# Routing steps tied to the low part of their tile, twelve instead of eight up tiles split by GpSimd

## The chip, the cores and the metric

One core of a Trainium2 chip runs the whole program in one launch. The metric is device time in microseconds (us), the median of several executions; less is better. The engines are named as the profile names them: PE is TensorE (matmuls), DVE is VectorE, ACT is ScalarE, POOL is GpSimd, SP issues the loads. PEld is PE's weight load.

## The reference

A decoder trunk of two layers on 256 tokens with 1024 channels: layer 0 mixes by retention, layer 1 by sparse attention, and each layer ends with a product-key expert network ("peer") of 16384 experts. The change is in that network alone:

```python
q = (xc @ w_q).reshape(T, 8, 2, 128)
s = einsum('thcd,hcnd->thcn', q, sub_keys)      # 8 heads, 2 halves, 128 keys
sv, si = top_k(s, 16)
comb = (sv[:, :, 0, :, None] + sv[:, :, 1, None, :]).reshape(T, 8, 256)
cv, ci = top_k(comb, 16)
eidx = i1 * 128 + i2        # i1, i2: si taken at ci // 16 and ci % 16
w = softmax(cv)
a = gelu(einsum('td,thkd->thk', xc, u_tab[eidx])) * w
y = einsum('thk,thkd->td', a, v_tab[eidx])
```

## The kernel before

All matrix products are made in three passes. Each fp32 operand is split into a high part, rounded by ACT (`hi`, line 98), and a low part, the difference `lo = raw - hi` (function `minus`, line 105), and `mm3` sums high by high, high by low and low by high.

The expert network doesn't gather. It goes through all 128 tiles of 128 experts: `up(i)` multiplies the tokens with tile i of `u_tab` (24 matmuls of 256 columns), a gelu makes `g`, DVE multiplies it by the dense routing weight `W`, and `down(i)` multiplies the result with tile i of `v_tab`. The tiles come in two halves of 64; in each, `RING` = 60 up tiles run first. The network runs twice, once a layer; below these are the first and the second network.

In the first 60 up tiles of the first half, DVE and ACT also finish the routing:

- `queries` and `first` (before the up tiles): scores and the two top-16 lists of each head; `second` (lines 593 to 604): the top 16 of their sums. All are DVE work.
- `weights` (line 649 on DVE, then line 651, an exp on ACT that needs a table load before it, and one back for the gelu): the softmax's numerators, issued after up tile `FINISH[0]`.
- `ranks` (lines 618 to 643): which keys the winners have. 18 steps of small and large DVE instructions, dealt out over the up tiles of `RANKS`.
- `normalised` (lines 656 to 659), then `finish` after up tile `FINISH[1]`: six transposes on PE, copies by ACT.
- `dense` (lines 689 to 700): 34 steps dealt out over the up tiles of `DENSE`; DVE makes one-hot rows, PE multiplies them, ACT copies them into `W`.

`UPLO` says for each up tile which engine makes its two low parts: "pp" is POOL, "dd" is DVE. `hi` and `lo` have four buffers each, two tiles' worth, so ACT and the engine of the low part run at most two tiles ahead of PE; the raw tiles have five.

PE's order is the order in which the code is written. On DVE, ACT and POOL a scheduler orders the instructions by its own estimates, except inside `manual_schedule`, and `issue_after(x)` keeps what stands in it behind instruction x in that order. Each engine works its list strictly in order.

Of the kernel before, what the change touches and what calls it, by code (L numbers as in the profile page):

```python
# [16 lines left out]
OP = mybir.AluOpType  # L17
# [7 lines left out]
HALF = 64  # L25
RING = 60
TB = 8
UPLO = (["pp"] * 8 + ["dd"] * 52, ["dd"] * 60)
DENSE = (24, 59), (0, 56)
FINISH = (8, 23)  # L30
RANKS = (9, 22)
STEPS = [1] * 4 + [2, 0, 0] * 5 + [2, 1] * 6 + [2]
WSCALE = 2.0 ** 14
C_ADAB, C_KVB, C_LNG, C_LNB, C_B1, C_PE, C_END = 0, 96, 112, 144, 176, 180, 212
# [3 lines left out]
def trunk(ctx, tc, a, out, dbg=None, stop=None):  # L38
    nc = tc.nc
# [24 lines left out]
    state = {}  # L64
# [4 lines left out]
    def x_tile():  # L69

        state["x"] = const.tile([P, 2, D], FT, tag="x", name="x")
        return state["x"]
# [29 lines left out]
            nc.gpsimd.tensor_scalar(dst, src, 1.0, 0.0, op0=OP.mult, op1=OP.add)  # L102

    def minus(eng, dst, x, y):
        (nc.vector if eng == "dve" else nc.gpsimd).tensor_tensor(dst, x, y, op=OP.subtract)  # L105

    def part512(raw, n, lo):

# [49 lines left out]
    def drain(g, n=10 ** 9):  # L158
        for _ in range(n):
            if next(g, StopIteration) is StopIteration:  # L160
                return
# [346 lines left out]
    def peer(l, h2, g, bg, end=lambda norm: iter(())):  # L508
        V = nc.vector
        with ExitStack() as s:  # L510
# [104 lines left out]
            def ranks(tt):  # L615

                for c in range(2):
                    V.tensor_copy(sf[:, tt, c], si[:, tt, :, c].rearrange("p h j -> p j h"))

                p, q, r0, r1 = cf[:, tt, 0], cf[:, tt, 1], rr[:, tt, 0], rr[:, tt, 1]  # L620
                V.tensor_copy(p, ci[:, tt].rearrange("p h k -> p k h"))
                V.tensor_scalar(ci[:, tt], ci[:, tt], 3, None, op0=OP.logical_shift_right)
                V.tensor_copy(r0, ci[:, tt].rearrange("p h k -> p k h"))
                V.tensor_scalar(r0, r0, -1.0, 0.0, op0=OP.add, op1=OP.max)
                V.tensor_scalar(q, p, 16.0, -8.0, op0=OP.is_ge, op1=OP.mult)
                yield
                V.scalar_tensor_tensor(r1, r0, -8.0, p, op0=OP.mult, op1=OP.add)
                V.tensor_tensor(r1, r1, q, op=OP.add)
                V.tensor_scalar(q, p, 72.0, None, op0=OP.is_lt)
                V.tensor_tensor(r1, r1, q, op=OP.mult)  # L630
                V.tensor_scalar(q, p, -72.0, 0.0, op0=OP.add, op1=OP.max)
                V.tensor_tensor(r0, r0, q, op=OP.add)
                yield
                for c in range(2):
                    o = one[:, c]
                    V.tensor_tensor(o, iota8[:, :, None, :].to_broadcast([P, 16, 16, 8]),
                                    rr[:, tt, c, None].to_broadcast([P, 16, 16, 8]), op=OP.is_equal)
                    yield
                    V.tensor_tensor(o, o, sf[:, tt, c, :, None].to_broadcast([P, 16, 16, 8]), op=OP.mult)
                    yield  # L640
                    for n in (8, 4, 2):
                        V.tensor_tensor(o[:, 0:n], o[:, 0:n], o[:, n:2 * n], op=OP.add)
                    V.tensor_tensor(route[:, tt, 1 + c], o[:, 0], o[:, 1], op=OP.add)
                    yield

            def weights():
                w = route[:, :, 0]
                for tt in range(2):
                    V.tensor_tensor(w[:, tt], cv[:, tt].rearrange("p h k -> p k h"),
                                    cv[:, tt, None, :, 0].to_broadcast([P, 16, 8]), op=OP.subtract)  # L650
                nc.scalar.activation(w, w, AF.Exp)
# [25 lines left out]
            def dense(tt, half):  # L677

                if tt == 0:
                    W[half] = sb.tile([P, HALF, T], FT, tag="w", name="W")  # L680
                w = W[half][:, :, tt * P:tt * P + P]

                def rows(n):
                    t0 = tt * P + n * TB
                    pairs = lambda x: x.rearrange("p t (n y) -> p t n y", y=2)
                    bc = lambda x, m: x[:, t0:t0 + TB, None, :].to_broadcast([P, TB, m // 2, 2])
                    count = lambda o, m: pairs(iota[:, None, o:o + m].to_broadcast([P, TB, m]))
                    oA, hi, lo = pairs(ohA[n % 2]), pairs(ohB[n % 2][:, 0]), pairs(ohB[n % 2][:, 1])
                    V.tensor_tensor(oA, count(0, P), bc(i2, P), op=OP.is_equal)  # L689
                    V.tensor_tensor(lo, count(half * HALF, HALF), bc(i1, HALF), op=OP.is_equal)  # L690
                    V.tensor_tensor(hi, lo, bc(wp[:, 0], HALF), op=OP.mult)
                    V.tensor_tensor(lo, lo, bc(wp[:, 1], HALF), op=OP.mult)

                def products(n):
                    ps = bank("aux").rearrange("p (t b) -> p t b", b=HALF)
                    for t in range(TB):
                        for x in range(2):
                            nc.tensor.matmul(ps[:, t], ohA[n % 2][:, t], ohB[n % 2][:, x, t],  # L698
                                             start=(x == 0), stop=(x == 1))
                    nc.scalar.activation(w[:, :, n * TB:n * TB + TB].rearrange("p b t -> p t b"), ps, AF.Copy,  # L700
                                         scale=1.0 / WSCALE)

                for n in range(P // TB):
                    rows(n)
                    if n:
                        products(n - 1)
                    yield
                products(P // TB - 1)
                yield
# [3 lines left out]
            def up(i, lo):  # L713
                if i % 2 == 0:
                    G["ps"] = bank("mm").rearrange("p (a t) -> p a t", t=T)
                proj(G["ps"][:, i % 2], split(load(a["peer_u"][l, i]), lo=lo), h2)
                if i % 2:
                    gt = tok.tile([P, 2, T], FT, tag="g", name="g", bufs=RING // 2)
                    G["last"] = nc.scalar.activation(gt, G["ps"], AF.Gelu_apprx_tanh)
                    G[i // 2] = gt  # L720
# [44 lines left out]
            for half in range(2):  # L765
                base = half * HALF
                steps = (x for tt in range(2) for x in dense(tt, half))
                ranking = (x for tt in range(2) for x in ranks(tt))
                for i in range(RING):
                    if half and i % 2:  # L770
                        drain(bg, 1)
                    up(base + i, UPLO[half][i])
                    if half == 0 and i == FINISH[0]:

                        with tc.issue_after(G["last"].ins):
                            weights()
                    if half == 0:
                        lo, hi = RANKS
                        due = lambda i: (min(max(i, lo), hi) - lo) * 18 // (hi - lo)
                        drain(ranking, due(i + 1) - due(i))  # L780
                    if half == 0 and i == FINISH[1] - 1:
                        drain(ranking)
                        normalised()
                    if half == 0 and i == FINISH[1]:
                        finish(0)
                        finish(1)
                    lo, hi = DENSE[half]
                    due = lambda i: (min(max(i, lo), hi) - lo) * 34 // (hi - lo)
                    drain(steps, due(i + 1) - due(i))
                drain(steps)  # L790
                for i in range(HALF - 4 * half):
                    if i % 2 or half == 0 and i % 8 == 0:
                        drain(bg, 1)
                    down(base + i, "dd")
                    if i % 2 and RING + i < HALF + 1:
                        up(base + RING + i - 1, "dd")
                        up(base + RING + i, "dd")
                    if half and i == 40:

                        nc.sync.dma_start(x_tile(), kept)  # L800
                        alloc = lambda: tok.tile([P, 512], FT, tag="g", name="row", bufs=RING // 2)
                        residual(2 * l, alloc)
                    if half and i == HALF - 8:
                        drain(bg)
                        norm = Norm(gate_rows(g, alloc), alloc)
                        ending = end(norm)
                        drain(ending, 1)
# [325 lines left out]
    if stop == "ret":  # L1133
        return
    norm = peer(0, h2, 40, bg1())
    h4 = nsa(norm, bg2())
    if stop == "peer0":
# [95 lines left out]
```

## Time and profile before

| | |
|---|---|
| median of 3 runs | 2101.12 us (2097.2 to 2110.17) |
| the profiled execution | 2099.38 us, its span 2097.2 us |
| PE busy | 2023.5 us, 96% |
| DVE / ACT / POOL busy | 78% / 58% / 8% |
| mean granted TensorE clock | 0.988 of 2.4 GHz |

The span is from the first to the last instruction; 2.18 us of the execution lie around it. PE is the engine that sets the end, so what a stage costs is read from PE's gaps and from the spacing of its matmuls.

### The profile page before, as it was taken

What the parts mean: (1) busy time and instruction counts of PE and PEld (TensorE: products, weight loads), DVE (VectorE), ACT (ScalarE), POOL (GpSimd) and SP (SyncE); (2) the same over time, 40 slices, a digit from 0 to 9 for tenths busy, and PEclk for the clock granted to TensorE, in tenths of its full rate; (3) what the DMA queues carried; (4) which work ended last, traced back from release to release, by engine and by line L of the source; (5) the groups of instructions that cost most, each with busy time, mean ns of one, the idle gap of its engine ahead of it and who ended that gap; (6) DMA issues with size and microseconds to landing.
All of it is one profiled execution on the core that took longest, in us unless ns stands there. A gap on an engine that the chain in (4) does not pass through costs nothing.

```text
span 2097.2 us, 39708 instructions
## 1 busy us (share of the span) xinstructions
PE 2023.5 (96%) x14658; PEld 1810.2 (86%) x14658; DVE 1637.4 (78%) x3812; ACT 1217.1 (58%) x2154; POOL 160.9 (8%) x182
## 2 busy tenths in 40 slices
PE   7999989999999999999989999899999999999997
PEld 6898889998777999977779679899977889998886
DVE  7898697989876778887684877978996667779666
ACT  4565555776555666655554565467655556665554
POOL 0000560000000000000010327200000000000000
PEclk9999999999999999999999999999999999999999
DMA  9877645546777766777656545454576655556664
GB/s 330 305 244 236 207 142 171 162 153 213 241 236 238 214 206 209 220 243 231 214 171 217 179 132 162 132 181 153 180 222 200 189 183 166 167 181 203 189 191 141
DMA packets 116466, 417.05 MB, mean 199 GB/s; under 512 B 13072, under 2 KB 14640, under 8 KB 115376
## 3 DMA queue, kind: packets, MB, share of 16 engines
q1 hardware_dynamic: 115264, 411.90, 61.6%
q10 hardware_dynamic: 1008, 2.63, 0.4%
q8 instruction: 114, 1.87, 0.3%
q14 instruction: 80, 0.66, 0.1%
HBM read 411.31 MB, written 3.16 MB: 198 GB/s over the span
## 4 chain that ended last, share of the span: by engine, by line
PE 76%; DVE 13%; DMA 5%; issue 3%; ACT 1%; POOL 1%; DVEq 0%; SPq 0%; ACTq 0%; POOLq 0%
PE mm L131 13%; PE mm L133 13%; PE mm L132 13%; PE acc L133 10%; PE acc L132 10%; PE acc L131 10%; DMA raw<-in_ada_w 4%; DVE lo L105 3%; PE aux L698 3%; DVE raw L151 1%; DVE raw L322 1%; PE aux L893 1%; DMA raw<-in_kv_ada_w 1%; ACT hi L98 1%; DVE g L727 1%
## 5 line engine op out<-in xcount | busy, mean ns | idle before, releaser
L98 ACT ACTIVATE hi<-raw 128x512 fp32r<-128x512 f32 x1272 | 799.2, 632 | 759.3 <-PE acc L133 352.2
L105 DVE TENSOR_TENSOR lo<-raw,hi 128x512 fp32r<-128x512 f32 x1184 | 800.7, 688 | 314.7 <-ACT hi L98 311.0
L133 PE MATMUL mm<-hh,lo 128*128 128x256 f32 x2528 | 716.0, 283 | 20.5 <-DVE lo L105 20.5
L131 PE MATMUL mm<-hh,hi 128*128 128x256 f32 x2528 | 729.0, 288 | 0.0
L132 PE MATMUL mm<-hl,hi 128*128 128x256 f32 x2528 | 714.5, 283 | 1.5 <-POOL hl L105 1.4
L133 PEld LDWEIGHTS mm<-hh,lo 128*128 128x128 f32 x2528 | 479.5, 190 | 21.6 <-DVE lo L105 21.5
L132 PEld LDWEIGHTS mm<-hl,hi 128*128 128x128 f32 x2528 | 480.0, 190 | 3.0 <-POOL hl L105 2.1
L131 PEld LDWEIGHTS mm<-hh,hi 128*128 128x128 f32 x2528 | 480.0, 190 | 0.8
L133 PE MATMUL acc<-hi,a 128*128 128x512 f32 x992 | 394.7, 398 | 6.7 <-DVE a L105 6.7
L132 PE MATMUL acc<-lo,a 128*128 128x512 f32 x992 | 393.0, 396 | 2.3 <-DVE lo L105 2.2
L131 PE MATMUL acc<-hi,a 128*128 128x512 f32 x992 | 392.3, 395 | 0.0
L133 PEld LDWEIGHTS acc<-hi,a 128*128 128x128 f32 x992 | 186.3, 188 | 60.3 <-DVE a L105 16.4
L132 PEld LDWEIGHTS acc<-lo,a 128*128 128x128 f32 x992 | 186.4, 188 | 50.1 <-DVE lo L105 6.0
L131 PEld LDWEIGHTS acc<-hi,a 128*128 128x128 f32 x992 | 186.4, 188 | 43.1
L151 DVE SCALAR_TENSOR_TENSOR raw<-raw,crow 128x1024 f32<-128x1024 f32 x96 | 117.2, 1222 | 62.9 <-DMA raw<-in_ada_w 53.2
L700 ACT ACTIVATE W<-aux 128x512 f32<-128x512 f32 x128 | 142.7, 1115 | 0.0
L105 POOL TENSOR_TENSOR lo<-raw,hi 128x512 fp32r<-128x512 f32 x88 | 113.4, 1300 | 24.7 <-ACT hi L98 21.2
L105 DVE TENSOR_TENSOR a<-g,a 128x256 fp32r<-128x256 f32 x248 | 103.6, 419 | 0.0
L98 ACT ACTIVATE a<-g 128x256 fp32r<-128x256 f32 x248 | 99.6, 403 | 1.8 <-DVE g L727 1.8
L727 DVE TENSOR_TENSOR g<-g,W 128x256 f32<-128x256 f32 x256 | 94.7, 420 | 0.8 <-ACT W L700 0.8
L689 DVE TENSOR_TENSOR hot<-iota,i 128x1024 f16<-128x1024 f16 x128 | 87.6, 685 | 0.0
L698 PE MATMUL aux<-hot 128*128 128x64 f16 x2048 | 82.0, 194 | 0.0
(265 smaller groups left out, 1836.1 us busy)
## 6 DMA issues: line engine op xcount, KB each, us to landing
raw<-in_peer_u SPq DMA_DIRECT2D x256, 512.0 KB, 3.7
raw<-in_peer_v SPq DMA_DIRECT2D x256, 512.0 KB, 4.3
raw<-in_ada_w SPq DMA_DIRECT2D x96, 512.0 KB, 4.5
raw<-in_ret_in SPq DMA_DIRECT2D x32, 512.0 KB, 4.5
raw<-in_peer_q SPq DMA_DIRECT2D x32, 512.0 KB, 4.2
raw<-in_ret_qk SPq DMA_DIRECT2D x16, 512.0 KB, 5.8
raw<-in_ret_o SPq DMA_DIRECT2D x16, 512.0 KB, 4.2
raw<-in_kv_ada_w SPq DMA_DIRECT2D x16, 512.0 KB, 4.2
```

Of the source, the lines that this page charges most:

```text
L98: nc.scalar.activation(dst, src, AF.Copy)
L105: (nc.vector if eng == "dve" else nc.gpsimd).tensor_tensor(dst, x, y, op=OP.subtract)
L131: nc.tensor.matmul(ps, sh, mh, start=start, stop=False, skip_group_check=True)
L132: nc.tensor.matmul(ps, sh, ml, start=False, stop=False, skip_group_check=True)
L133: nc.tensor.matmul(ps, sl, mh, start=False, stop=stop, skip_group_check=True)
L151: nc.vector.scalar_tensor_tensor(raw, raw, 1.0, crow, op0=OP.mult, op1=OP.mult, accum_out=mod[:, o + j:o + j + 1])
L322: nc.vector.scalar_tensor_tensor(raw, raw, 1.0, crow, op0=OP.mult, op1=OP.mult, accum_out=mod[:, o + k:o + k + 1])
L689: V.tensor_tensor(oA, count(0, P), bc(i2, P), op=OP.is_equal)
L698: nc.tensor.matmul(ps[:, t], ohA[n % 2][:, t], ohB[n % 2][:, x, t], start=(x == 0), stop=(x == 1))
L700: nc.scalar.activation(w[:, :, n * TB:n * TB + TB].rearrange("p b t -> p t b"), ps, AF.Copy, scale=1.0 / WSCALE)
L727: V.tensor_tensor(gi, gi, W[half][:, i % HALF], op=OP.mult)
L893: nc.tensor.matmul(ps[:, 64 * f:64 * f + 60], w1[:, jj, f * P:f * P + P], zp[:, j], start=(j == 0 and f == 0), stop=(j == 15 and f == 1), ...
```

## The change

Four tables move and one binding is added. POOL makes the low parts of up tiles 0 to 11 instead of 0 to 7; the softmax numerators are issued after up tile 11 instead of 8, the transposes after tile 25 instead of 23; the rank steps are dealt over tiles 12 to 24 instead of 9 to 22, the one-hot steps over tiles 26 to 59 instead of 24 to 59. And `minus` remembers the last low part that DVE was given, and each rank step is put behind it: the low part of the tile at which the step is due.

```diff
-UPLO = (["pp"] * 8 + ["dd"] * 52, ["dd"] * 60)
-DENSE = (24, 59), (0, 56)
-FINISH = (8, 23)
-RANKS = (9, 22)
+UPLO = (["pp"] * 12 + ["dd"] * 48, ["dd"] * 60)
+DENSE = (26, 59), (0, 56)
+FINISH = (11, 25)
+RANKS = (12, 24)
@@ minus
-        (nc.vector if eng == "dve" else nc.gpsimd).tensor_tensor(dst, x, y, op=OP.subtract)
+        ins = (nc.vector if eng == "dve" else nc.gpsimd).tensor_tensor(dst, x, y, op=OP.subtract)
+        if eng == "dve":
+            state["low"] = ins
@@ peer
-                        drain(ranking, due(i + 1) - due(i))
+                        with tc.issue_after(state["low"].ins):
+                            drain(ranking, due(i + 1) - due(i))
```

Below, tile 8 of the first network is the one with raw_3643 before, and tile 12 the one with raw_3788 after; `big` holds the scores and the routing. Line numbers after are two higher from line 106 on (four from the rank loop on). On DVE before, from the last step of `second` to the first low parts that DVE makes of up tiles (left out are fourteen more small rank instructions):

```order
L604 MAX_INDEX big_2486<-big_2486 128x8
L649 TENSOR_TENSOR big_2486<-big_2486 128x128
L623 CAST big_2486<-big_2486 128x128
...
L636 TENSOR_TENSOR big_2486<-iota8_85,big_2486 128x2048
L632 TENSOR_TENSOR big_2486<-big_2486 128x128
L639 TENSOR_TENSOR big_2486<-big_2486 128x2048
L105 TENSOR_TENSOR lo_3646<-raw_3643,hi_3645 128x512
L636 TENSOR_TENSOR big_2486<-iota8_85,big_2486 128x2048
L105 TENSOR_TENSOR lo_3650<-raw_3643,hi_3649 128x512
L639 TENSOR_TENSOR big_2486<-big_2486 128x2048
```

The same place after:

```order
L606 MAX_INDEX big_2486<-big_2486 128x8
L651 TENSOR_TENSOR big_2486<-big_2486 128x128
L105 TENSOR_TENSOR lo_3791<-raw_3788,hi_3790 128x512
L105 TENSOR_TENSOR lo_3795<-raw_3788,hi_3794 128x512
L620 CAST big_2486<-big_2486 128x128 x2
...
L105 TENSOR_TENSOR lo_3832<-raw_3829,hi_3831 128x512
L626 TENSOR_SCALAR big_2486<-big_2486 128x128
L105 TENSOR_TENSOR lo_3836<-raw_3829,hi_3835 128x512
...
L638 TENSOR_TENSOR big_2486<-iota8_85,big_2486 128x2048
L105 TENSOR_TENSOR lo_3876<-raw_3873,hi_3875 128x512
```

All rank steps that stood ahead of the first low part now stand behind it, and the low parts of a tile are followed by that tile's steps. On ACT before, at the exp of the softmax:

```order
L719 ACTIVATE g_3640<-mm_3571 128x512
L651 ACT_TABLE_LOAD
L651 ACTIVATE big_2486<-big_2486 128x2x128
L98 ACTIVATE hi_3726<-raw_3724 128x512
L98 ACTIVATE hi_3730<-raw_3724 128x512
```

And after:

```order
L721 ACTIVATE g_3782<-mm_3713 128x512
L653 ACT_TABLE_LOAD
L653 ACTIVATE big_2486<-big_2486 128x2x128
L98 ACTIVATE hi_3875<-raw_3873 128x512
L98 ACTIVATE hi_3879<-raw_3873 128x512
```

The exp stood behind the gelu of tiles 6 and 7, ahead of the high parts of tile 10; now it stands behind that of tiles 10 and 11, ahead of those of tile 14.

## Rows read from the trace of the kernel before

**Rows 1.** PE's waits over the span: who, for whom, us in total, times, longest.

```profile
PE mm L133 <- DVE lo L105: 23.0, 7, 9.2
```

**Rows 2.** PE in order of time, first network: start, length, line, idle before and releaser.

```profile
308.13 0.28 PE L132 MATMUL mm<-hl,hi 128*128 128x256 f32 x1
317.33 0.58 PE L133 MATMUL mm<-hh,lo 128*128 128x256 f32 x1 [8.93 <-DVE lo L105]
317.71 0.41 PE L131 MATMUL mm<-hh,hi 128*128 128x256 f32 x1
...
321.53 0.28 PE L131 MATMUL mm<-hh,hi 128*128 128x256 f32 x1
```

**Rows 3.** The same of the second network.

```profile
1340.39 0.58 PE L133 MATMUL mm<-hh,lo 128*128 128x256 f32 x1 [9.18 <-DVE lo L105]
...
1345.59 0.28 PE L133 MATMUL mm<-hh,lo 128*128 128x256 f32 x1
```

**Rows 4.** Stretches: length, busy (count) of PE, PEld, DVE, ACT, POOL; clock; DMA share; GB/s.

```profile
309.00:318.00 9.00, 0.67 (x3) 0.67 (x4) 9.00 (x45) 1.96 (x3) 0.00 (x0) 0.62 0.00 0
318.00:351.00 33.00, 33.00 (x265) 32.81 (x265) 28.41 (x57) 17.20 (x28) 0.00 (x0) 0.95 0.60 179
...
366.00:480.00 114.00, 114.00 (x1313) 112.66 (x1312) 102.55 (x203) 81.77 (x122) 0.00 (x0) 1.00 0.52 162
```

**Rows 5.** ACT in order of time: gelus of tile pairs, a high part, the exp.

```profile
308.14 0.63 ACT L98 ACTIVATE hi<-raw 128x512 fp32r<-128x512 f32 x1 [0.82 <-PE mm L132]
308.68 0.58 ACT L719 ACTIVATE g<-mm 128x512 f32<-128x512 f32 x1
309.28 1.28 ACT L651 ACT_TABLE_LOAD   x1
312.18 0.42 ACT L651 ACTIVATE big<-big 128x256 f32<-128x256 f32 x1 [1.62 <-DVE big L649]
...
342.68 0.58 ACT L719 ACTIVATE g<-mm 128x512 f32<-128x512 f32 x1
...
348.38 0.58 ACT L719 ACTIVATE g<-mm 128x512 f32<-128x512 f32 x1
...
1331.50 0.58 ACT L719 ACTIVATE g<-mm 128x512 f32<-128x512 f32 x1
...
1360.37 0.58 ACT L719 ACTIVATE g<-mm 128x512 f32<-128x512 f32 x1
...
1366.13 0.58 ACT L719 ACTIVATE g<-mm 128x512 f32<-128x512 f32 x1
```

**Rows 6.** DVE in order of time, first network.

```profile
299.30 1.28 DVE L594 TENSOR_TENSOR big<-big 128x224 f32<-128x224 f32 x1
...
301.76 1.42 DVE L618 CAST big<-big 128x128 f16<-128x128 uint32 x1
...
307.12 0.36 DVE L594 TENSOR_TENSOR big<-big 128x224 f32<-128x224 f32 x1
...
311.79 0.35 DVE L649 TENSOR_TENSOR big<-big 128x128 f32<-128x128 f32 x1
312.06 0.25 DVE L623 CAST big<-big 128x128 f16<-128x128 uint32 x1
...
316.59 0.68 DVE L105 TENSOR_TENSOR lo<-raw,hi 128x512 fp32r<-128x512 f32 x1
317.19 1.22 DVE L636 TENSOR_TENSOR big<-iota,big 128x2048 f16<-128x2048 f16 x1
...
340.97 1.29 DVE L105 TENSOR_TENSOR lo<-raw,hi 128x512 fp32r<-128x512 f32 x2
```

**Rows 7.** DVE's low parts from 312.06 to 341.6: count, busy us, mean ns, idle.

```profile
L105 DVE TENSOR_TENSOR lo<-raw,hi 128x512 fp32r<-128x512 f32 x19 | 12.7, 684 | 0.0
```

**Rows 8.** POOL's low parts from 286 to 304.4, where they end, and all (min/median/max ns).

```profile
L105 POOL TENSOR_TENSOR lo<-raw,hi 128x512 fp32r<-128x512 f32 x12 | 15.4, 1300 | 4.2 <-ACT hi L98 4.1
...
L105 POOL TENSOR_TENSOR lo<-raw,hi x88: 1269/1291/1472, 235.5 to 1326.0; 128x512 fp32r<-128x512 f32 x88
```

## The prediction

> **What bounds the kernel now.** I read PE's waits first, then the places where they fall, then who was late there. PE is busy 96% of the span, so only its gaps and slow matmuls are to be had. The largest group of its waits is for low parts made by DVE, 23.0 us in 7 waits [rows 1]; two of them are nearly all of it, 8.93 and 9.18 us, one in each expert network [rows 2, 3]. In order of time both stand at the same instruction: the third matmul of up tile 8, the first that reads a low part from DVE instead of POOL.
>
> The wait is not the whole loss. In the stretch from 309 to 318 the granted clock falls to 0.62 [rows 4], and the matmuls after the gap start 0.212 us apart (18 of them from 317.71 to 321.53 [rows 2]), where those of an undisturbed pair of tiles start 0.119 apart (48 in 5.70 us [rows 5]): half the full level, 1.2 for 2.4 GHz, after an engine that had stood still. The loss with both parts in it is read from ACT's gelus, one for each pair of tiles. First network: from 308.68 to 342.68 there are four pairs in 34.00 us; at 5.70 (348.38 less 342.68) they take 22.80, so 11.2 us are lost. Second: 1331.50 to 1366.13 is 34.63, less 4 x 5.76 (1366.13 less 1360.37) is 11.6 [rows 5]. Together 22.8 us is the most the change can take out here.
>
> Who was late: DVE, without a pause. It ends the routing's last top-16 step and the softmax's second subtraction at 312.1, then runs rank steps, and gives tile 8 its first low part only at 316.59 [rows 6]. PE had wanted it at 308.25, 0.12 us after its last matmul of tile 7 [rows 2]. So 3.9 us of the wait are the top-16 work and 4.5 us are rank steps ordered ahead of a low part; the low part itself and the way to PE make the rest.
>
> **The change part by part.**
>
> *Four more tiles by POOL.* DVE's first low part is due four tiles later: PE starts tile 12 at 308.2 + 4 x 2.87 = 319.7 (2.87 is half of 5.70 to 5.76 [rows 5]). POOL makes sixteen low parts more, eight in each network. It takes 1.30 each, 15.4 us for 12, and in that stretch it waited 4.2 us, nearly all for ACT's high parts [rows 8]; PE uses a half tile in 1.43. So POOL keeps pace with 0.13 to spare and can be priced at nothing: what hides it is PE itself, which frees the buffers that ACT waits for (the high part at 308.14 was released by PE [rows 5]). If the cover were gone, each 0.1 us over 1.43 would cost 1.6 us over sixteen halves. There is a rule against this part: the Trainium skill (GPSIMD Engine Reference, § 4.1 Engine selection) puts elementwise work with two inputs on VectorE, GpSimd being about twice as slow. The rows agree, 1300 ns against 684 [rows 7, 8]. By the page's factor of two the half would take an estimated 1.37, still under 1.43, and the sum would stay.
>
> *DVE beside POOL.* POOL's last low part ended at 304.4 [rows 8]; now it works until about 316. That lies on top of DVE's last top-16 work, and the rows show what such a meeting costs: the 224-column add took 1.28 at 299.30, while POOL worked, and 0.36 at 307.12, after it; the cast at 301.76 took 1.42, one of the same size at 312.06 took 0.25 [rows 6]. Five additions and subtractions of this kind lie in the new overlap (three of `second`, two of `weights`). The bounds are nothing and the 0.92 of the pair just named for each, 4.6 us in all. I take the upper, as the nearest row. On the other side, the rank casts that stood before 312.1 now come behind tile 12's low part: about 1.2 (1.42 less 0.25) and 0.7 for four small ones leave. The top-16 work then ends at 312.1 - 1.9 + 4.6 = 314.8, or at 310.2 without meetings. Either way it is before 319.7. The Trainium skill (SBUF — State Buffer, § Who interferes with whom) says that a DVE instruction with two SBUF inputs and a GpSimd instruction lock each other out for a whole instruction, whichever came first. The 1.28 against 0.36 agrees. By that rule the worst is an estimated five POOL instructions, 6.5 us, and the end is 316.6, still ahead of tile 12.
>
> *Rank steps behind their tile.* Before, the steps ran ahead of the low parts. Now DVE's list is low parts of tile 12, its steps, low parts of tile 13, and so on. Tile 12's first low part can't start before its high part: that needs the buffer which tile 10 frees half through, at 308.2 + 5.7 + 1.43 = 315.4, and 0.63 on ACT, so 316.1 [rows 5]. It is ready at 316.8 and due at 319.9: DVE enters with 3.1 us in hand. What it has to do in tiles 12 to 23: from 312.06 to 342.2 it was never idle, 30.1 us, of which nineteen low parts at 0.60 (their spacing when in a row) are 11.4 [rows 6, 7]; the rest, 18.7, and the 0.7 above are 19.4 us of rank work. With 24 low parts that is 19.4 + 14.4 = 33.8 us, against 12 x 2.87 = 34.4 of PE. It fits, closely. The steps aren't even: adding up the new order tile by tile, tile 19 has 4.3 us and tile 21 4.2 (each holds an equality and a product of 1.14 to 1.22 beside its low parts), and they use up the 3.1 in hand: tile 22's first low part comes just when PE wants it. I take 0.3 us of waiting per network for that; the bounds are 0 and 1.5, the latter if DVE enters 3 us late.
>
> *The exp on ACT.* It moves with its two table loads of 1.28 to the end of tile 11. Before, PE's wait hid them. Now they come at about 320.4, and the high part of tile 14, possible from about 321.3, starts at 322.1 instead, ready 0.8 us late with 2.7 in hand before tile 14. So nothing, hidden by ACT's two tiles of lead; if that lead were used up, 3 us per network.
>
> *Transposes and one-hot steps.* They come two tiles later in the code and earlier on the clock (tile 26 at 359.9; tile 24 was at 365). The 34 one-hot steps now share 33 tiles instead of 35. In that stretch PE was busy 114.00 of 114 and DVE 102.55 [rows 4]; 6% more one-hot work per tile lifts both, PE by its products, and DVE stays under 95%. The number of instructions is the same, so nothing. The new first one-hot rows stand ahead of tile 28's low parts, with about 1 us in hand.
>
> *Sixteen low parts off DVE* (0.60 each, 9.6 us) come off an engine that does not set the end outside the two places above: nothing more. SP's loads keep their order.
>
> **The sum.** 22.8 less 2 x 0.3 and 0.3 for POOL's tiles at the slower of the two pair times is 21.9 us. The profiled execution took 2099.4 with what lies around its span, which gives 2077.5; it lay 1.7 below the median of the three runs. Against the median: 2101.1 - 21.9 = **2079**.
>
> **The rivals.**
>
> *The wait moves.* DVE enters tile 12 late, or the lumps in tiles 19 to 22 cost more, and PE stands still again for 3 us or more and falls to half level. Price: 3 to 5 us of waiting, and as after the old gap some 4.2 us at 0.212 instead of 0.119, which is 1.9: 5 to 7 per network, 12 together, so about 2091. For it: 33.8 of 34.4 us is a narrow fit, and DVE's spacing could be longer beside POOL. Against: POOL is done by 316, and after the old gap DVE interleaved rank steps and low parts for 24 us with no further PE wait.
>
> *Slower than before: POOL becomes the bound.* In tiles 8 to 11 POOL and DVE's two-input work meet; if each of POOL's halves stood behind DVE as that add stood behind POOL, several times over, PE would wait at each half. All 22.8 us are gone when the sixteen halves lose 1.43 each, that is at 2.7 us on POOL; at 3.2 the time is some 8 us over the old, 2109. Against: of 88 such instructions the slowest took 1472 ns, although DVE was at work beside them [rows 8].
>
> *It doesn't do what it says.* The steps are off PE's path, but PE meets the same lateness at the transposes in tile 26, and the time stays near 2100. Before, DVE had the rank work done at 342, over 20 us ahead of the transposes; now about 352 against 360. There is room, so this is unlikely.
>
> **How the numbers follow.** Forecast 0.73; the wait that moves 0.19; no effect 0.04; slower 0.04. The forecast's own range is a gain of 19 to 24, with the medians of three runs some 4 us uncertain: 2073 to 2085. The range is drawn to 2093 so that most of the first rival is in it, **2073 to 2093**. About 1%, 21 us, is what a measurement of this kernel can tell from none, and the sum lies right on it: of the forecast's 0.73, some 0.53 fall over it. So faster by over 1% 0.53, within 1% 0.44 (the rest of the forecast, the moved wait, and most of the no-effect cases), slower 0.03.
>
> **What would show it.** In the changed profile the two long waits for DVE's low part are gone from PE's list and the clock stays at 1.00 over the stretch from 300 to 360; the gelus come every 5.7 us through tiles 6 to 24; DVE idles before tile 12's low part for ACT, at about 316; POOL's low parts run to about 316 at 1.3 us. I'm wrong if PE waits for a low part at tile 12 or at tiles 19 to 22 for over 2 us, if POOL's low parts grow past 1.43, if the exp delays tile 14, or if a gap opens elsewhere, at the transposes or where the first down tile starts.

## The result, and the profile after

The changed kernel takes 2079.07 us (median of 6 runs, 2077.22 to 2082.07), the kernel before 2101.25 in 6 runs beside it (2093.97 to 2110.17). The ratio is 0.9896, with a 95% interval of 0.9881 to 0.991: faster by 1.04%. The change is small, but the interval lies wholly below 1. The profiled execution took 2077.25 us, its span 2075.5, at a clock of 0.992.

PE's waits over the whole span of the changed kernel, two of its groups (who, for whom: total us, times, longest); [rows 1] had 23.0 us in 7 waits, the longest 9.2, where the second of these stands:

```profile
PE acc L133 <- ACT hi L98: 12.8, 8, 11.2
...
PE mm L135 <- DVE lo L105: 6.2, 6, 1.9
```

The first stood in the kernel before as well (12.6 us in 7) and belongs to other stages. The waits for DVE's low parts lost 16.8 us and both long ones. Two stretches of the changed kernel (length, busy and count of PE, PEld, DVE, ACT, POOL; clock; DMA share; GB/s), to be held against [rows 4]:

```profile
300.00:360.00 60.00, 59.33 (x500) 59.13 (x500) 52.67 (x161) 33.87 (x55) 15.66 (x12) 1.00 0.63 187
360.00:474.00 114.00, 114.00 (x1326) 112.66 (x1325) 102.73 (x203) 82.55 (x123) 0.00 (x0) 1.00 0.53 163
```

PE stands still for 0.67 us in the whole stretch, and the clock is at its full level throughout. ACT of the changed kernel in order of time: the gelus of tiles 6 and 7, 10 and 11, the exp behind its table load, the gelus of 14 and 15, 20 and 21, 22 and 23; then the first and the last of the four pairs in the second network:

```profile
309.41 0.58 ACT L721 ACTIVATE g<-mm 128x512 f32<-128x512 f32 x1
...
320.80 0.58 ACT L721 ACTIVATE g<-mm 128x512 f32<-128x512 f32 x1
321.40 1.28 ACT L653 ACT_TABLE_LOAD   x1
322.69 0.42 ACT L653 ACTIVATE big<-big 128x256 f32<-128x256 f32 x1
...
332.13 0.58 ACT L721 ACTIVATE g<-mm 128x512 f32<-128x512 f32 x1
...
349.22 0.58 ACT L721 ACTIVATE g<-mm 128x512 f32<-128x512 f32 x1
...
355.85 0.58 ACT L721 ACTIVATE g<-mm 128x512 f32<-128x512 f32 x1
...
1323.34 0.58 ACT L721 ACTIVATE g<-mm 128x512 f32<-128x512 f32 x1
...
1346.06 0.58 ACT L721 ACTIVATE g<-mm 128x512 f32<-128x512 f32 x1
```

The four pairs that took 34.00 and 34.63 us [rows 5] take 22.72 in both networks: 11.3 and 11.9 us less, 23.2 together. The exp no longer waits for DVE (there is no bracket behind it). The gelu right behind it, of tiles 12 and 13, comes 1.35 us late (327.85), the next is on its mark again, and PE doesn't wait. The one irregular pair is 349.22 to 355.85: 6.63 instead of 5.70, so 0.9 us go back there (6.64 in the second network). PE in order of time shows why:

```profile
348.72 0.28 PE L134 MATMUL mm<-hl,hi 128*128 128x256 f32 x1
349.67 0.39 PE L135 MATMUL mm<-hh,lo 128*128 128x256 f32 x1 [0.67 <-DVE lo L105]
349.89 0.28 PE L133 MATMUL mm<-hh,hi 128*128 128x256 f32 x1
```

It is the first low part of tile 22. From 349.89 on, the matmuls behind this wait are 0.12 us apart, at full rate, unlike those of [rows 2]. On DVE of the changed kernel, from the last routing sum (`second`'s additions) on:

```profile
306.41 0.26 DVE L595 TENSOR_TENSOR big<-big 128x64 f32<-128x64 f32 x1
...
306.82 1.45 DVE L596 TENSOR_TENSOR big<-big 128x224 f32<-128x224 f32 x1
308.19 1.30 DVE L599 TENSOR_TENSOR big<-big 128x32 f32<-128x32 f32 x1
309.42 0.37 DVE L651 TENSOR_TENSOR big<-big 128x128 f32<-128x128 f32 x1
...
313.67 0.37 DVE L651 TENSOR_TENSOR big<-big 128x128 f32<-128x128 f32 x1
...
316.65 0.69 DVE L105 TENSOR_TENSOR lo<-raw,hi 128x512 fp32r<-128x512 f32 x1 [2.62 <-ACT hi L98]
318.08 0.69 DVE L105 TENSOR_TENSOR lo<-raw,hi 128x512 fp32r<-128x512 f32 x1 [0.73 <-ACT hi L98]
...
320.93 0.69 DVE L105 TENSOR_TENSOR lo<-raw,hi 128x512 fp32r<-128x512 f32 x1 [0.33 <-ACT hi L98]
...
346.46 1.22 DVE L638 TENSOR_TENSOR big<-iota,big 128x2048 f16<-128x2048 f16 x1
347.79 1.22 DVE L641 TENSOR_TENSOR big<-big 128x2048 f16<-128x2048 f16 x1
348.93 1.29 DVE L105 TENSOR_TENSOR lo<-raw,hi 128x512 fp32r<-128x512 f32 x2
```

The routing ends at 314.0, DVE then idles 2.62 us until ACT has the high part of tile 12 (1.20 in the second network), and 0.73 and 0.33 us more for later high parts of tiles 12 and 13. The two long rank steps stand right ahead of tile 22's low parts. POOL of the changed kernel, its last sixteen low parts in the first network:

```profile
294.93 21.65 POOL L105 TENSOR_TENSOR lo<-raw,hi 128x512 fp32r<-128x512 f32 x16 [1.14 <-ACT hi L98]
```

They end at 316.6. They start 1.35 us apart on average, and the last of them 1.42, the pace at which PE takes half tiles.

Where the 21.7 us of the two spans (2097.2, 2075.5) are, by these marks: the two stages give 23.2, the waits at tile 22 take back 1.9. The rest, 0.4 us, is a sum of larger pieces in parts that the change doesn't touch: the first network's tiles 6 and 7 come 0.7 later, the way from one network to the other is 1.5 longer, and what follows tile 15 of the second network 2.6 shorter (without the waits at tile 22). Other executions scatter by as much and more: the gelu of tiles 6 and 7 in the first network came between 306.4 and 311.2, and at 306.4 in a second profile of the changed kernel itself.

### The profile page after: what moved, and what is told of

It is laid out like the page before. It is cut to its first block, busy times and chain, and to the rows that moved or that the text cites. A ratio compares the mean times of both kernels' runs of the same rounds, so it can differ in the third digit from the quotient of the medians.

```text
span 2075.5 us, 39708 instructions
## 1 busy us (share of the span) xinstructions
PE 2019.1 (97%) x14658; PEld 1805.4 (87%) x14658; DVE 1631.0 (79%) x3796; ACT 1216.5 (59%) x2154; POOL 182.3 (9%) x198
## 4 chain that ended last, share of the span: by engine, by line
PE 77%; DVE 12%; DMA 6%; issue 4%; ACT 1%; POOL 1%; DVEq 0%; SPq 0%; ACTq 0%; POOLq 0%
PE mm L133 14%; PE mm L135 14%; PE mm L134 14%; PE acc L135 10%; PE acc L134 9%; PE acc L133 9%; DMA raw<-in_ada_w 5%; DVE lo L105 4%; PE aux L700 3%; DVE g L729 1%; DVE raw L324 1%; DVE raw L153 1%; PE aux L897 1%; DMA raw<-in_kv_ada_w 1%; PE aux L577 1%
## 5 line engine op out<-in xcount | busy, mean ns | idle before, releaser
L105 DVE TENSOR_TENSOR lo<-raw,hi 128x512 fp32r<-128x512 f32 x1168 | 789.7, 688 | 302.8 <-ACT hi L98 299.4
L105 POOL TENSOR_TENSOR lo<-raw,hi 128x512 fp32r<-128x512 f32 x104 | 134.3, 1303 | 25.3 <-ACT hi L98 19.4
```

The lines of the kernel that those rows point to most:

```text
L105: ins = (nc.vector if eng == "dve" else nc.gpsimd).tensor_tensor(dst, x, y, op=OP.subtract)
```

## The experiments

The theory: three pieces are needed together (a *pair* below is a pair of up tiles, timed from gelu to gelu). POOL's tiles put off DVE's first low part, the binding keeps rank steps from running ahead of it, and the later exp keeps ACT's high parts from waiting for DVE. The rivals: the tables alone would do it, the binding alone would do it, or POOL is a free helper of which more is better.

**Tables without the binding.** All tables as changed, but rank steps free to go anywhere:

```diff
-                        with tc.issue_after(state["low"].ins):
-                            drain(ranking, due(i + 1) - due(i))
+                        drain(ranking, due(i + 1) - due(i))
```

> The changed tables without the binding. In its order nearly all of the rank work (some 17 of 19.4 us) stands ahead of the first low part that DVE makes, that of tile 12. Theory (the binding carries the gain, the four POOL tiles only move the place at which DVE is due): DVE ends the softmax subtraction at about 314, gives the low part at about 331, PE wanted it at 320: 11 us of waiting and some 2 at half clock in each network, 26 together, so about 2079 + 26 = 2105, no faster than before. Rival (what counts is that POOL covers DVE's last top-16 work for four tiles and takes 16 low parts off DVE): about 2079 to 2083.

Measured: 2111.51 us (2105.95 to 2114.12), ratio 1.0051 [1.0029, 1.0072]: slower than the kernel before. PE of this kernel, the first matmul of tile 12 that reads a low part:

```profile
334.85 0.58 PE L135 MATMUL mm<-hh,lo 128*128 128x256 f32 x1 [14.41 <-DVE lo L105]
```

DVE of this kernel, the end of the routing and the first low part:

```profile
317.04 0.36 DVE L651 TENSOR_TENSOR big<-big 128x128 f32<-128x128 f32 x1
...
319.49 1.22 DVE L638 TENSOR_TENSOR big<-iota,big 128x2048 f16<-128x2048 f16 x1
...
334.11 0.68 DVE L105 TENSOR_TENSOR lo<-raw,hi 128x512 fp32r<-128x512 f32 x1
```

DVE was free of the top-16 work at 317.3, which would have been in time for tile 12; then it ran 16.8 us of rank steps ahead of the low part. Four tiles more for POOL move the meeting from tile 8 to tile 12, and the list of rank steps that stands ahead of it grows with the room. The four pairs from 320.72 to 359.55 lose 16.0 us, more than the 11.2 before. The theory's wait of 11 us was too small, though it had the rank steps right (some 17 us; 16.8 measured): it had the softmax subtraction end at 314, and it ended at 317.4. Rank casts stood among the top-16 work there and met POOL's low parts (one took 0.82 us instead of some 0.26), and the routing stood 1.2 us later against PE than in the profile after the change. That the tables alone would do it is out.

**The binding alone.** Old tables, the binding kept:

```diff
-UPLO = (["pp"] * 12 + ["dd"] * 48, ["dd"] * 60)
-DENSE = (26, 59), (0, 56)
-FINISH = (11, 25)
-RANKS = (12, 24)
+UPLO = (["pp"] * 8 + ["dd"] * 52, ["dd"] * 60)
+DENSE = (24, 59), (0, 56)
+FINISH = (8, 23)
+RANKS = (9, 22)
```

> The binding with the tables of before (eight POOL tiles). Theory: of the old 9 us wait the 4.5 of rank steps go, what stays is the top-16 work that ends at 310.2 (2.0 us sooner, as the rank casts are no longer mixed in) and the low part, due at 308.3: some 2.5 to 3 us of waiting in each network, and the clock either stays or falls for some 4 us (1.9). So 2079 + 2 x 2.7 to 2079 + 2 x 4.6: 2084 to 2088. Rival (the POOL tiles carry the gain): about 2100.

Measured: 2086.47 us (2083.08 to 2088.86), ratio 0.9932 [0.9908, 0.9955]. PE of this kernel at tile 8:

```profile
311.15 0.58 PE L135 MATMUL mm<-hh,lo 128*128 128x256 f32 x1 [4.56 <-DVE lo L105]
311.53 0.42 PE L133 MATMUL mm<-hh,hi 128*128 128x256 f32 x1
...
316.66 0.35 PE L133 MATMUL mm<-hh,hi 128*128 128x256 f32 x1
```

DVE of this kernel there:

```profile
310.14 0.35 DVE L651 TENSOR_TENSOR big<-big 128x128 f32<-128x128 f32 x1
310.41 2.49 DVE L105 TENSOR_TENSOR lo<-raw,hi 128x512 fp32r<-128x512 f32 x4
```

The low part follows the top-16 work at once, and what is left is the part of the wait that no order of the rank steps can take: 4.56 and 4.48 us. The theory had 2.5 to 3, with the top-16 work 2.0 us sooner once no rank casts stand in it. Against PE it came no sooner: the last subtraction ended 3.8 us after PE's last matmul before the wait, in the kernel before 3.7 (second network: 3.7 and 3.9). In the first network the casts had gone, but the routing stood later against PE: from the first 64-column sum of the last `second` to the gelu of tiles 6 and 7 it is 8.3 us here, and 9.7 before. In the second it is 8.3 in both, but the casts there were short (0.27 us, where one took 1.42 in the first [rows 6]).

From 311.53 to 316.66 PE ran its 24 matmuls 0.214 us apart. The four pairs take 30.04 and 30.07 us, so 7.2 are lost in each network instead of 11.2 and 11.6. Against 34.00 and 34.63 that is 8.5 us of gain. The spans differ by 10.6 and the medians by 13.2. The 2.1 us between 8.5 and 10.6 are scatter outside the two stages: the first one begins 1.8 us sooner, the way between the networks is 1.6 longer, and what follows is 1.8 shorter. So the median, inside its forecast of 2084 to 2088, hides that each network lost more at tile 8 than the 2.7 to 4.6 us of the theory. The binding alone isn't enough. The rest of the gain needs POOL's tiles and the later exp, which this run takes back together.

**Ten tiles by POOL, not twelve.** The other tables follow by as much:

```diff
-UPLO = (["pp"] * 12 + ["dd"] * 48, ["dd"] * 60)
-DENSE = (26, 59), (0, 56)
-FINISH = (11, 25)
-RANKS = (12, 24)
+UPLO = (["pp"] * 10 + ["dd"] * 50, ["dd"] * 60)
+DENSE = (24, 59), (0, 56)
+FINISH = (9, 23)
+RANKS = (10, 22)
```

> The changed kernel with ten POOL tiles instead of twelve and everything after two tiles sooner (rank steps over 10 to 22, transposes after 23). Theory: DVE's first low part is due at 314.2 and the softmax subtraction ends at 314.0, so the low part comes at 314.7: about 0.5 us late, and DVE then has nothing in hand for the uneven tiles, which cost 1 to 3 us more in each network: 2080 to 2085. With twelve DVE idles 2.6 us there, so eleven would be enough. Rival (twelve tiles are needed, since POOL's relief of DVE is the gain): 2088 or more.

Measured: 2083.92 us (2081.93 to 2086.78), ratio 0.9929 [0.9906, 0.9953]. DVE of this kernel, the end of the routing and tile 10's low parts:

```profile
313.06 0.36 DVE L651 TENSOR_TENSOR big<-big 128x128 f32<-128x128 f32 x1
313.34 1.28 DVE L105 TENSOR_TENSOR lo<-raw,hi 128x512 fp32r<-128x512 f32 x2
```

DVE comes to tile 10 without having idled, so it enters the rank steps with nothing in hand, and the pairs of tiles 16 to 21 run at 6.00, 6.16 and 6.84 us instead of 5.70 (gelus at 332.29, 338.29, 344.45, 351.29). With 0.7 us at tile 10 that is 2.6 us per network, where twelve tiles lose 0.9. The time is as forecast (2080 to 2085). What the last two tiles of POOL buy is DVE's lead, not the end of a long wait.

**Rank and one-hot steps spread wider.** The changed kernel with two tiles more for the rank steps:

```diff
-DENSE = (26, 59), (0, 56)
-FINISH = (11, 25)
-RANKS = (12, 24)
+DENSE = (28, 59), (0, 56)
+FINISH = (11, 27)
+RANKS = (12, 26)
```

> The changed kernel with the rank steps dealt over tiles 12 to 26, the transposes after tile 27, the one-hot steps over tiles 28 to 59. Theory (the one wait that is left, 0.95 us at tile 22 in each network, is DVE's uneven load in tiles 19 to 21): it goes, PE's gelus come every 5.7 us to the transposes, 1.9 us less, 2077. The price would be one-hot steps that are too dense for DVE (34 over 31 tiles, DVE at some 95%). Rival (the wait is something else, such as the raw tile or the high part): it stays, 2079.

Measured: 2078.92 us (2074.95 to 2082.66), ratio 0.99 [0.9873, 0.9928]. PE had no wait for a low part from 300 to 360 nor from 1290 to 1380, and the gelus come every 5.70 us up to the transposes: the waits at tile 22 came from the dealing. The time doesn't show it. So it was run again, beside the changed kernel as it is, in five rounds:

> The kernel with the rank steps dealt over tiles 12 to 26 once more, beside the changed kernel: no wait at tile 22, so 1.9 us less than that one, 0.09%, which five rounds may just tell. Rival: the saved wait comes back elsewhere, as in the denser one-hot steps, and both are equal.

> The changed kernel itself once more, beside the next one on the same chip: 2079, PE's wait at tile 22 of 0.67 us in each network (0.95 with the spacing).

Measured: 2076.83 (2075.59 to 2083.02) for the spread, ratio 0.9891 [0.9871, 0.991]; 2077.3 (2075.59 to 2081.45) for the changed kernel, ratio 0.9892 [0.9874, 0.991]. The spans of the profiled executions are 2074.3 and 2075.5. The medians can't confirm a gain of 1.9 us. The gelus show where it goes: from tiles 6 and 7 to tiles 58 and 59 the spread takes 166.96 and 167.02 us, the changed kernel beside it 167.79 and 167.81. So 1.6 of the 1.9 us are kept there, and a little comes back in the one-hot stretch, where two pairs take 7.28 instead of 6.81, as the rival has it.

**The exp after tile 8 as before.** The changed kernel with one number back:

```diff
-FINISH = (11, 25)
+FINISH = (8, 25)
```

> The changed kernel with the exp of the softmax where it was before, behind the gelu of tiles 6 and 7. Theory: ACT then stands at the exp until VectorE ends the softmax subtraction at 314.0, where it would have gone on at 310.3; the high part of tile 10 comes 4.1 us late, and GpSimd's low part behind it at 316.4, due at 314.9: 1.5 to 2.5 us per network, 2082 to 2084. So moving the exp is a needed part of the change. Rival (ACT's lead of two tiles hides it): 2079.

Measured: 2082.69 us (2079.89 to 2087.82), ratio 0.9918 [0.9895, 0.9941]; its span is 2079.2. ACT of this kernel in order of time:

```profile
307.93 0.58 ACT L721 ACTIVATE g<-mm 128x512 f32<-128x512 f32 x1
308.53 1.28 ACT L653 ACT_TABLE_LOAD   x1
312.58 0.42 ACT L653 ACTIVATE big<-big 128x256 f32<-128x256 f32 x1 [2.77 <-DVE big L651]
312.90 2.17 ACT L98 ACTIVATE hi<-raw 128x512 fp32r<-128x512 f32 x4
```

PE of this kernel, in tile 10:

```profile
313.57 0.38 PE L133 MATMUL mm<-hh,hi 128*128 128x256 f32 x1 [0.47 <-ACT hi L98]
...
314.92 0.39 PE L135 MATMUL mm<-hh,lo 128*128 128x256 f32 x1 [0.85 <-POOL lo L105]
```

The exp needs DVE's second subtraction, and ACT works in order: four high parts queue up behind an exp that waits 2.77 us (4.17 in the second network), POOL gets them late, and PE runs dry. The two pairs around it lose 1.8 us together in the first network and 3.3 in the second (the theory had 1.5 to 2.5). So the place of the exp carries some 4 us of the gain (3.7 by the spans, 5.4 by the medians). The two ratios' intervals overlap, so the figure rests on the profile, not on the times.

**More for POOL.** The changed kernel, with POOL making the low part of the first half of each of tiles 12 to 24 as well, beside the rank steps on DVE:

```diff
-UPLO = (["pp"] * 12 + ["dd"] * 48, ["dd"] * 60)
+UPLO = (["pp"] * 12 + ["pd"] * 13 + ["dd"] * 35, ["dd"] * 60)
```

> The changed kernel in which GpSimd also makes the first low part of each of the tiles 12 to 24, so that VectorE is relieved of 13 x 0.6 = 7.8 us in each network while it does the rank steps. Theory (a VectorE instruction with two inputs beside a GpSimd instruction waits for its end, as the 224-column add did: 1.45 instead of 0.36): GpSimd works 45% of the time there, some 45 of the rank instructions and low parts are two-input ones or casts, and each that meets it loses some 0.6 to 1.1: 12 us or more, above the 7.8 saved. VectorE falls behind, and PE waits for low parts: 2 to 6 us per network, 2083 to 2091. Rival (the relief is worth more than the meetings, as the tile 22 wait was one of load): the wait at tile 22 goes, 2077.

Measured: 2093.16 us (2090.93 to 2095.84), ratio 0.9956 [0.994, 0.9973]: 15.9 us slower than the changed kernel beside it and above the 2083 to 2091 of the theory, though 13 low parts of 0.60 us left DVE in each network. DVE by line and shape from 318 to 352, of this kernel (count, busy us, mean ns, idle before):

```profile
L641 DVE TENSOR_TENSOR big<-big 128x2048 f16<-128x2048 f16 x3 | 5.7, 1901 | 0.0
L644 DVE TENSOR_TENSOR big<-big 128x1024 f16<-128x1024 f16 x3 | 4.2, 1403 | 0.0
...
L625 DVE CAST big<-big 128x128 f16<-128x128 uint32 x2 | 1.6, 806 | 0.0
```

The same view of the changed kernel:

```profile
L641 DVE TENSOR_TENSOR big<-big 128x2048 f16<-128x2048 f16 x4 | 4.9, 1218 | 0.0
L644 DVE TENSOR_TENSOR big<-big 128x1024 f16<-128x1024 f16 x4 | 2.7, 686 | 0.0
...
L625 DVE CAST big<-big 128x128 f16<-128x128 uint32 x2 | 0.5, 272 | 0.0
```

A stretch of the kernel with more on POOL, to be read like those above:

```profile
332.00:362.00 30.00, 25.45 (x197) 23.87 (x198) 29.52 (x47) 12.05 (x20) 12.93 (x8) 1.00 0.47 141
```

Its PE waits over the span:

```profile
PE mm L135 <- DVE lo L105: 15.8, 21, 1.2
```

DVE is now busy for 29.52 of 30 us and sets the pace: pairs take 7.20 to 7.39 us. POOL's low parts grew as well, 12.93 us for eight. A DVE instruction that begins while one of POOL's is under way is longer by about as much as POOL still needs, as here:

```profile
347.10 1.80 POOL L105 TENSOR_TENSOR lo<-raw,hi 128x512 fp32r<-128x512 f32 x1 [2.46 <-ACT hi L98]
...
347.79 2.19 DVE L641 TENSOR_TENSOR big<-big 128x2048 f16<-128x2048 f16 x1
```

POOL was done at 348.90, and the product, 1.22 long by itself, at 349.98. The Trainium skill (SBUF — State Buffer, § Who interferes with whom) has the two lock each other out for whole instructions where DVE reads two SBUF inputs; these durations agree. That POOL is a free helper is out. In tiles 8 to 11 it was nearly free; DVE spent that time on maxima, index searches and replacements, which took 0.22 to 0.29 us each beside it. That this is the reason is read from the durations; no run changes it alone.

## Why the prediction was right

**The loss of 22.8 us.** It was read from the gelus of before, and 23.2 came back by the same marks, 0.4 more than "the most": the four pairs take 5.68 each in both networks, also where the prediction allowed 5.76. That the wait was top-16 work and rank steps in about equal parts is borne out: with the binding alone 4.56 and 4.48 us of wait are left, and 4.4 and 4.7 go. That the figures agree so closely is partly luck, since the 3.9 us of top-16 work had rank casts in it. One slip changes no number: the matmul at 308.13 in [rows 2] is the second of tile 8, not the last of tile 7.

**POOL's tiles at nothing.** Right: 1.30 us each, the slowest of all 104 at 1.48, and no PE wait in tiles 8 to 11 of either network. The rule of the Trainium skill against two-input work on GpSimd (GPSIMD Engine Reference, § 4.1 Engine selection) is decided by place: 15.9 us of loss beside the rank steps, none beside the top-16 work. The 0.3 us at the slower pair time did not come.

**DVE beside POOL.** The upper bound of 4.6 us, five waits, was too high. Two of the five instructions waited: the 224-column addition (1.45, against 0.36 in [rows 6]) and the one behind it, 1.30; with 0.37 for either subtraction and 0.26 for the 64-column addition little or nothing was added there. Counted from the first 64-column sum of the last `second` (298.96 before, 299.94 after), the last subtraction ended 0.9 us later than before, where the prediction's terms made it 2.7. It decided nothing, since DVE then idled for ACT, as foreseen (316.65, for about 316).

**Rank steps behind their tile.** They fit, though narrowly: PE waits at one place only, and it is the place that the prediction named, tile 22. The size was off. Instead of 0.3 us per network it costs 0.9, inside the bounds of 0 and 1.5. This is the term of the sum that was mis-sized, by 1.3 us in all. DVE entered with the lead foreseen (tile 12's first low part done at 317.3, wanted at some 320.5), but the sum of 33.8 us counts DVE's work alone. The trace shows it idle for 0.73 and 0.33 us after it had entered, because its next low parts stood ahead of the rank steps and their high parts weren't there yet. That is 1.06 us of lead used up, more than the wait of 0.67. No run takes these two waits out, so that they made the difference is not shown.

**The exp.** Nothing, as said: it ran at 322.69 without a wait, with the high parts of tile 14 right behind it at 323.02, and PE didn't wait. The prediction should have said what it was worth to move it: its table load and its wait were hidden by the old gap, and the run with the exp left in its place shows 4 us of loss once that gap is gone.

**Transposes, one-hot steps, loads.** Nothing, as said: PE is busy 114.00 of 114 us there and DVE 102.73, and the gelus from tiles 22 and 23 to tiles 58 and 59 take 121.37 us, 0.25 more than before.

**The sum.** 23.2 less 1.9 is 21.3, the sum of the prediction 21.9, the profiled executions 22.1 apart. So the mechanism holds, and the sum to 0.6 us. That the median hit 2079 to 0.1 us is luck: six runs of this kernel spread over 4.9 us, and a loss 0.4 larger than counted made up for part of a lump 1.3 larger. The rival of the moved wait didn't come, but its price was nearly right: the binding alone shows a wait of 4.56 us that costs 7.2 in each network, just over its 5 to 7, since PE ran at half rate for 5.1 us behind it and not for 4.2.

## What to carry to other kernels

When an in-order engine makes operands for PE, bind its background work behind the operand that is due and give the foreground operands away for as long as the background's first part lasts: here the binding alone gave 8.5 of the 21.3 us net that the gelus show (13 of 22 by the medians), and the give-away alone made the kernel slower. Before work goes to GpSimd, look at what VectorE does in the same stretch: beside maxima and index searches it cost nothing, beside two-input arithmetic more than it took over. When a long wait is removed, list what it had hidden on each engine (here the exp on ACT), since that is what is late next.

## What the runs showed of the hardware

The clock and the gaps: after 4.56 us of standing still PE ran 24 matmuls at half rate (0.214 us apart instead of 0.12; the granted clock was 0.51 from 311.15 to 316.90). How long it stayed there didn't grow with the gap: 18 such steps after 8.93 us [rows 2]. In the run with more for POOL, 4.55 us of idle time in 30 us, in waits of at most 1.15, left the granted clock at 1.00, and so did the 0.67 us at tile 22 and, in the run with the early exp, waits of 1.86 and 0.85 us within 7. Short waits aren't cheap for that: in the run with more for POOL, four pairs with some 4.5 us of waits lost 6.5 us (29.33 for 22.8), against 7.2 for the one wait of 4.56.

Where a DVE instruction with two inputs and a low part on POOL met, the one that began first ran through in these rows, and the other waited. POOL's low parts beside two additions and the two subtractions of the changed kernel:

```profile
306.74 1.28 POOL L105 TENSOR_TENSOR lo<-raw,hi 128x512 fp32r<-128x512 f32 x1
308.15 1.30 POOL L105 TENSOR_TENSOR lo<-raw,hi 128x512 fp32r<-128x512 f32 x1
309.58 1.37 POOL L105 TENSOR_TENSOR lo<-raw,hi 128x512 fp32r<-128x512 f32 x1
...
313.85 1.35 POOL L105 TENSOR_TENSOR lo<-raw,hi 128x512 fp32r<-128x512 f32 x1
```

The additions at 306.82 and 308.19 began 0.08 and 0.04 us after one of them and ended 0.25 and 0.04 us behind it. The subtractions at 309.42 and 313.67 began ahead of one, took 0.37 us, no more than alone, and it was POOL that took 1.37 and 1.35 instead of 1.29. An instruction with one input can wait as well: in the run with more for POOL a cast grew to 806 ns in the mean, from 272.

The pairs of tiles take 5.70 us in most stretches and 5.76 in some, in several kernels and not always in the same stretch (the second network's before the change, the run with the early exp). No wait stands beside it, and its cause is open.
